# A hybrid decoder block on one core: the first shift and scale as products of raw weight blocks, and finer steps in the plan

## The chip, the cores and the metric

The kernel runs on one core of a Trainium2 chip. The metric is the device time of one execution in microseconds (us); lower is better. The kernel before took 2522.41 us, the median of 3 runs (2518.33 to 2524.78). Engines are named as the profile does: PE is TensorE (products and transposes), DVE is VectorE, ACT is ScalarE, POOL is GpSimd, and SP issues the DMA transfers.

## The reference

One layer of a decoder: 1024 tokens, 1024 channels, all in float32.

```python
mod = (silu(c) @ w_ada + b_ada)[:, None, :]            # w_ada: 1024 x 6144
sh1, sc1, gt1, sh2, sc2, gt2 = split(mod, 6)
h = rms_norm(x, norm1_w) * (1 + sc1) + sh1
q, kv, nsa_g, z, xbc, dt_raw, mg = split(h @ w_in, IN_OFFSETS)
o_attn = nsa_attention(q, kv...)      # 16 heads, 2 K/V groups: compressed, selected and window branch
o_ssm  = mamba2_mixer(z, xbc, dt_raw) # causal convolution of 4 taps over xbc, then the state space model
x = x + gt1 * ((g_attn * (o_attn @ w_attn_out) + g_ssm * (o_ssm @ w_ssm_out)) @ w_o)
h = rms_norm(x, norm2_w) * (1 + sc2) + sh2
x = x + gt2 * ((silu(h @ w_gate) * (h @ w_up)) @ w_down)   # w_gate, w_up: 1024 x 2816
return rms_norm(x, norm_f_w)
```

## The kernel before, in words

**Products.** To keep float32 accuracy a large product is taken as three: each operand is split into a high part (`hi`, a copy in the type fp32r) and a low part (`lo`, the rest), and `mm3k` issues hi·hi, hi·lo and lo·hi (L322 to L324). Making a `hi` costs an ACT copy, making a `lo` a subtraction on DVE or POOL. A few small products, and the transposes, use plain float32.

**Plan.** No engine's order is written by hand. `Flow` works out, while the program is built, when every operation would start. Each operation is queued with an engine, a cost in us, what it needs, and a function that issues it. `advance` takes from the queues of ACT, DVE, POOL and SP whatever can start first; `drive` does so for PE, choosing among streams (Python generators that yield one PE step at a time) the one that can start earliest, the first in the list at a tie. An entry whose function issues several instructions puts them in its engine's order together, with nothing between them. `first=True` puts an entry at the head of its queue. A change of one cost or one entry can thus move operations elsewhere. Buffers come from rings (`buf`, `until`): a buffer's next user waits for the operations named in `until`.

**Start.** `startup` loads the token tiles x (`xload`, eight of 512 KB), the blocks of `w_ada` that hold the first shift and scale (`wada`: halves h = 0 and 1 of the columns, eight blocks of 128 rows each), and the first weights (`split`: a raw block of 512 KB, then hi and lo). Only the SP queue sets the transfers' order: x0, x1, the eight blocks of half 0, the first raw block of kv0 (columns of w_in for keys and values), the eight blocks of half 1, the second raw block of kv0, x2, x3, kv1, x4, x5, constants, x6, x7. DVE multiplies each arriving block by its entry of `sc` = silu(c) and adds it to `acc` (L449); when a half is summed, PE adds over the partitions by products with a tile of ones (`shift_scale`, L500, two steps of four products for each half), and DVE adds the bias (`ab`, L503). `norm1` takes the norm of a pair of token tiles and transposes it (L535). `modulate` applies shift and scale to a pair's transposed quarter (`tmp`), and casts it to hT_hi and hT_lo. `token_block` then makes kv and q: eight steps of three products for a token tile and a weight block (`tokps`), pairs of tiles in order. The later tiles x4 to x7 are loaded where blocks 4 to 7 of half 1 lay.

**Middle.** Attention takes 16 units for each K/V group; its PE steps come first, and `background` fills what is left of PE with the other projections (28 weight blocks: z, x and the merge gates), with their own convolution. For the x columns `finish_x` copies the product to `xr`, and applies the taps: one ACT operation and three on DVE (`conv`, L1165, one entry). `score_cmp` is the softmax of the compressed branch, with entries of three DVE, four ACT and three DVE instructions. `value_step` transposes probabilities and copies them as a hi and lo pair (`kv`, L2321 on ACT and L2322 on DVE), with which PE makes `o` (L1098). `w_sums` prepares sums of w_down blocks, stored to DRAM.

**Towards the FFN.** `out_proj` makes x + ..., tile by tile; `norm2` stores the tile to DRAM (`x1d`), takes its norm (the root on DVE, L293 to L296 and L269, L274), and `turn_x` transposes it and makes the sums of tokens and channels for the FFN (T1 to T4). The FFN's products are taken by a scheme of seven products for a 2 x 2 block product (`gate_up`, tiles `gu`), which needs seven sums of blocks of w_gate (or w_up) as hi and lo: `ff_raw` loads two raw blocks of 512 KB, `ff_pieces` makes the sums (L1772) and `part` their hi and lo (L1753 on ACT, L1755 on DVE or POOL). Products 1 and 2 need only what even token tiles give; 3 and 5 to 7 need the odd ones. For the first pair of columns (b = 0) pieces of w_gate come before the first product, pieces 1 and 2 of w_up through `ff_first`, and the rest of w_up at the fifth product (`n == 4`). Buffers named x1r, whi_pc and wlo_pc hold the pieces; M and E hold the tokens' blocks.

## Time and profile before

| | us |
|---|---|
| median of the runs | 2522.41 |
| the profiled execution | 2519.45 |
| its span, first to last instruction | 2517.6 |
| what lies around the span | 1.85 |
| PE's longest wait, for the first x tile (L535 for DVE's L525) | 17.4 |
| PE's waits for DVE's `kv` (L1098 and L1095 for L2322), 12 together | 12.4 |
| PE's waits for DVE's `sm` (L2233 for L2238), 3 together | 4.3 |
| PE's waits for `ab` (L500 for L503), 2 together | 2.4 |

The span is that of the profiled execution alone. A row of a timeline gives start, duration, engine, line, operation, output and inputs, how many instructions stand together, and in brackets the idle time before and what ended it. A row of a table by stage gives the stretch, its length, and for each engine the busy time with its number of instructions. PEclk (in tenths) and the granted clock (1.00 is full) are TensorE's; PEld are weight loads, which run beside the products. A wait row reads: who, waited for whom: us in total, times, the longest.

### The profile page before, as it was taken

How to read it: one execution, taken by the hardware profiler on the slowest of the kernel's cores; microseconds unless marked ns; L12 is line 12 of the kernel's file. 1: busy time of each engine (PE TensorE's matmuls, PEld its weight loads, DVE VectorE, ACT ScalarE, POOL GpSimd, SP SyncE). 2: the span in 40 equal slices, each digit the busy share in tenths (PEclk: the TensorE clock that was granted, in tenths of full speed). 3: DMA queues.
4: the chain of work that ended last, by engine and by line, in shares of the span. 5: the costliest groups of instructions: out<-in, count | busy, mean ns of one | idle time of the engine just before them, and what ended most of it. 6: DMA issues, size and time to landing. Idle time of an engine off the chain costs nothing. (4 is left out here: it accounts for less than half of the span.)

```text
span 2517.6 us, 39576 instructions
## 1 busy us (share of the span) xinstructions
PE 2432.4 (97%) x13674; PEld 2080.2 (83%) x13674; DVE 1794.7 (71%) x3910; ACT 1239.0 (49%) x2644; POOL 1165.1 (46%) x924
## 2 busy tenths in 40 slices
PE   5999999999999999999999999999989999999998
PEld 5999778898888888988877778778978888887886
DVE  7644787877776687875467886778787676765858
ACT  4422666666655576655556555532453323323543
POOL 2112474645555556455634342201255565665853
PEclk8999999999999999999999999999999999999999
DMA  7432443322335433333357876426422332326853
GB/s 251 131 125 86 152 120 95 92 92 89 98 103 167 128 114 97 93 105 101 99 188 231 263 233 193 148 73 227 150 80 96 109 105 92 110 91 235 309 167 117
DMA packets 267464, 349.74 MB, mean 139 GB/s; under 512 B 21368, under 2 KB 177784, under 8 KB 266752
## 3 DMA queue, kind: packets, MB, share of 16 engines
q1 hardware_dynamic: 267264, 347.21, 42.9%
q8 instruction: 108, 1.77, 0.3%
q14 instruction: 92, 0.75, 0.1%
HBM read 249.23 MB, written 97.91 MB: 138 GB/s over the span
## 5 line engine op out<-in xcount | busy, mean ns | idle before, releaser
L2251 POOL TENSOR_SCALAR P<-P,sm,gate 128x640 f32<-128x640 f32 (+7 forms) x256 | 215.4, 856 | 246.6 <-DVE sm L2248 200.0
L2322 DVE TENSOR_TENSOR kv<-tp,kv 128x512 fp32r<-128x512 f32 (+1 forms) x296 | 189.6, 656 | 108.9 <-ACT kv L2321 107.8
L2321 ACT ACTIVATE kv<-tp 128x512 fp32r<-128x512 f32 (+1 forms) x296 | 164.9, 573 | 185.5 <-PE tp L2318 177.6
L2242 ACT ACTIVATE P<-P,sm 128x640 f32<-128x640 f32 (+7 forms) x256 | 186.9, 732 | 47.2 <-DVE sm L2238 43.3
L1098 PE MATMUL o<-kv 128*128 128x512 f32 x528 | 189.4, 411 | 13.5 <-DVE kv L2322 9.4
L2233 PE MATMUL S<-kv,Q 128*128 128x384 f32 (+5 forms) x768 | 182.8, 337 | 4.3 <-DVE sm L2238 4.3
L2238 DVE CUSTOM_DVE_ANT_0 P<-S,kb 128x256 f32<-128x256 f32 (+5 forms) x256 | 120.3, 494 | 56.7 <-PE tp L2318 29.1
L322 PE MATMUL fps<-hT_hi,whi_x 128*128 128x512 f32 x384 | 157.7, 411 | 0.1
L1165 DVE SCALAR_TENSOR_TENSOR u<-xr,hcw,u 128x512 f32<-128x512 f32 x144 | 147.4, 1024 | 13.2 <-ACT u L1168 8.3
L2318 PE MATMUL tp<-id,P 128*128 128x128 f32 x1056 | 152.7, 273 | 0.6 <-POOL P L2251 0.6
L1887 DVE TENSOR_TENSOR ex<-ex,gu 128x512 f32<-128x512 f32 x122 | 82.0, 683 | 98.4 <-PE gu L324 95.4
L322 PE MATMUL fps<-whi_z,hT_hi 128*128 128x256 f32 x512 | 149.8, 293 | 1.5 <-DVE zu L1222 1.5
L324 PE MATMUL fps<-hT_hi,wlo_x 128*128 128x512 f32 x384 | 151.2, 394 | 0.0
L323 PE MATMUL fps<-hT_lo,whi_x 128*128 128x512 f32 x384 | 151.2, 394 | 0.0
L2318 PEld LDWEIGHTS tp<-id,P 128*128 128x128 f32 x1056 | 127.9, 141 | 21.2 <-POOL P L2251 0.8
L323 PE MATMUL fps<-wlo_z,hT_hi 128*128 128x256 f32 x512 | 144.4, 282 | 0.0
L324 PE MATMUL fps<-whi_z,hT_lo 128*128 128x256 f32 x512 | 144.4, 282 | 0.0
L2233 PEld LDWEIGHTS S<-kv,Q 128*128 128x128 f32 x768 | 128.3, 190 | 19.2 <-ACT P L2242 3.1
L1098 PEld LDWEIGHTS o<-kv 128*128 128x128 f32 x528 | 95.8, 189 | 35.1 <-DVE kv L2322 17.0
L1753 ACT ACTIVATE x1r<-ex 128x512 fp32r<-128x512 f32 x115 | 70.6, 626 | 104.7 <-POOL ex L1772 31.4
L1755 DVE TENSOR_TENSOR x1r<-ex,x1r 128x512 fp32r<-128x512 f32 x89 | 108.0, 1224 | 13.9 <-ACT x1r L1753 13.7
L2392 POOL TENSOR_TENSOR dx<-xs,hd 128x512 f32<-128x512 f32 x32 | 41.8, 1308 | 162.9 <-DVE yy L2434 124.5
(490 smaller groups left out, 8036.0 us busy)
## 6 DMA issues: line engine op xcount, KB each, us to landing
wada<-w_ada SPq DMA_DIRECT2D x40, 512.0 KB, 4.2
ex<-actd SPq DMA_DIRECT2D x70, 256.0 KB, 3.7
actd<-ex SPq DMA_DIRECT2D x69, 256.0 KB, 2.0
ac<-acd SPq DMA_DIRECT2D x32, 512.0 KB, 4.8
raw_x<-w_in SPq DMA_DIRECT2D x24, 512.0 KB, 4.3
ws<-w_down SPq DMA_DIRECT2D x44, 256.0 KB, 3.6
wsd<-ws SPq DMA_DIRECT2D x88, 128.0 KB, 1.8
ff<-w_gate SPq DMA_DIRECT2D x22, 512.0 KB, 5.0
```

The costliest lines, as they stand in the source:

```text
L322: mm(ps, lh, rh, start=k == 0, stop=False)
L323: mm(ps, lh, rl, start=False, stop=False)
L324: mm(ps, ll, rh, start=False, stop=k == kt - 1)
L1098: nc.tensor.matmul(o.t.rearrange("p h q -> p (h q)"), vst(), pair()[m], start=n + m == 0, stop=n == u.total - 1 and m == 1)
L1165: nc.vector.scalar_tensor_tensor(u.t, xr[:, k:k + N2], hcw[:, ft, k:k + 1], u.t, op0=OP.mult, op1=OP.add)
L2233: mm(sp[:, :w], q, kvb.kv[:, br, r, first + c0:first + c1], start=r == 0, stop=r == 1)
L2238: nc.vector.tensor_tensor_reduce(P[:, c0:c1], sp[:, :w], k.kb[:, m0:m0 + w], scale=-1.0, scalar=sm[:, 0, h:h + 1] if p else 3.0e38, op0=OP ...
L2242: ex = A(0.26 + 0.8333e-3 * n, [mx], lambda: nc.scalar.activation(P[:, :n], P[:, :n], AF.Exp, bias=sm[:, 1, h:h + 1], scale=-1.0, accum_ou ...
L2251: nc.gpsimd.tensor_scalar(P[:, :n], P[:, :n], sm[:, 3, m:m + 1], k.gate[:, i, self.h0 + m, br + 1:br + 2], op0=OP.mult, op1=OP.mult)
L2318: nc.tensor.transpose(tp[:, h * 128:h * 128 + 128], P, k.id)
L2321: hi = A(0.064 + 0.104 * n, [op, pair], lambda: nc.scalar.activation(pair()[0][:, c], tp[:, c], AF.Copy))
L2322: lo = V(0.068 + 0.133 * n, [hi], lambda: nc.vector.tensor_sub(pair()[1][:, c], tp[:, c], pair()[0][:, c]))
```

## The change

**Start.** The accumulation on DVE and ACT is gone. PE now takes products of each raw block of w_ada as it lands: eight of 128x128 weights (the block) with one moving column (`sc` of these rows), added up over the eight blocks of a half in one PSUM tile; DVE adds bias and norm weight once for each half. x2 and x3 are loaded before half 1 of w_ada instead of behind it: the SP order is x0, x1, half 0, kv0's first block, x2, x3, half 1, kv0's second block, kv1. kv0's second `lo` and the quarter p = 0, q = 0 of hT_lo move from POOL to DVE (`fast=2`; `if q == 1 and p`). `token_block` is cut into streams for pair 0, pair 1 and pairs 2 and 3, so that kv1's pair 0 can go before kv0's pair 1.

**Single operations.** The three taps of the convolution become three entries of the plan; so do the DVE and ACT operations of `score_cmp`.

**FFN.** The 14 first pieces (seven each of w_gate and w_up for b = 0) are made during the projections, after the weight blocks 21 and 22 of `background` (`ff_save`), and stored to DRAM (`pcd`, 28 stores of 256 KB); `gate_up` loads them (`ff_saved`, 28 loads). `ff_first` and the special case in `ff_pieces` go. The x1 store is put at the head of SP's queue.

PE's order at the start; adac is the tile of shift and scale, acc the sums, xT transposed tokens, wada and the like the raw blocks, tokps the token products. Before:

```order
L535 MATMUL xT<-id,xa 128x128 x12
L500 MATMUL adac<-ones,acc_125 128x64 x4
L535 MATMUL xT<-id,xa 128x128 x4
L500 MATMUL adac<-ones,acc_125 128x64 x4
L322 MATMUL tokps<-whi_kv_169,hT_hi 128x256
L323 MATMUL tokps<-wlo_kv_180,hT_hi 128x256
L324 MATMUL tokps<-whi_kv_169,hT_lo 128x256
```

After:

```order
L483 MATMUL adac<-sc,wada_116 128x1 x32
L521 MATMUL xT<-id,xa 128x128 x4
L483 MATMUL adac<-sc,wada_116 128x1 x16
L521 MATMUL xT<-id,xa 128x128 x4
L483 MATMUL adac<-sc,wada_116 128x1 x16
L521 MATMUL xT<-id,xa 128x128 x8
L483 MATMUL adac<-sc,wada_whi 128x1 x8
L322 MATMUL tokps<-whi_kv_231,hT_hi 128x256
L323 MATMUL tokps<-wlo_kv_245,hT_hi 128x256
L324 MATMUL tokps<-whi_kv_231,hT_lo 128x256
```

Half 0's products stand first now, with the transposes of tiles 0 and 1 among them. Of half 1, single blocks of eight products alternate with single token steps of three until half 1's eighth block; four steps in all come before its last 32 products. Before, L500 of half 1 (eight products) stood behind the first four steps.

DVE's order in attention, at the first head group of the first unit; u and xr are the convolution's buffers, Q the query tile, P and sm a branch's probabilities and sizes. Before:

```order
L1174 COPY tl<-xr 128x3
L1165 SCALAR_TENSOR_TENSOR u<-xr,hcw,u 128x512 x3
L1181 SCALAR_TENSOR_TENSOR u<-xr,u 128x512
L1178 COPY xr<-tl 128x3
L1165 SCALAR_TENSOR_TENSOR u<-xr,hcw,u 128x512 x3
L2196 TENSOR_TENSOR Q_0_0_2945<-tq_0_0_2935,Q_0_0_2945 64x256
L2197 TENSOR_TENSOR Q_0_0_2945<-tq_0_0_2935,Q_0_0_2945 64x256
L1181 SCALAR_TENSOR_TENSOR u<-xr,u 128x512
```

After:

```order
L1171 SCALAR_TENSOR_TENSOR u<-xr,u 128x512
L1166 COPY xr<-tl 128x3
L1153 SCALAR_TENSOR_TENSOR u<-xr,hcw,u 128x512
L2219 TENSOR_TENSOR Q_0_0_3032<-tq_0_0_3022,Q_0_0_3032 64x256
L2220 TENSOR_TENSOR Q_0_0_3032<-tq_0_0_3022,Q_0_0_3032 64x256
L1153 SCALAR_TENSOR_TENSOR u<-xr,hcw,u 128x512
L2261 ISA P_0_0_3072,sm_0_0_3027<-S_0_0_3063,kb 128x128
L2261 ISA sm_0_0_3027 128x1
L1153 SCALAR_TENSOR_TENSOR u<-xr,hcw,u 128x512
```

The taps stood as a block of three ahead of the query's operations; now the query and the first size stand between them.

DVE's order just before the FFN's first products; rq_n is a tile's root, ops and x_7 the output projection of tile 7, wlo_pc and x1r the low parts of FFN pieces. Before:

```order
L293 TENSOR_SCALAR rq_n_19712<-rq_n_19712 128x1
L294 TENSOR_SCALAR rq_n_19712<-rq_n_19712 128x1
L1755 TENSOR_TENSOR wlo_pc<-ex,whi_pc 128x512
L1622 TENSOR_TENSOR ops<-ops,sl 128x256
L1755 TENSOR_TENSOR wlo_pc<-ex,whi_pc 128x512
L1624 TENSOR_TENSOR x_7_18751<-x_7_18751,ops 128x256
L1755 TENSOR_TENSOR x1r_19760<-ex,x1r_19760 128x512
L1755 TENSOR_TENSOR x1r_19767<-ex,x1r_19767 128x512
L1622 TENSOR_TENSOR ops<-ops,sl 128x256
L296 TENSOR_SCALAR rq_n_19712<-rq_n_19712 128x1
```

After:

```order
L293 TENSOR_SCALAR rq_n_19892<-rq_n_19892 128x1
L294 TENSOR_SCALAR rq_n_19892<-rq_n_19892 128x1
L296 TENSOR_SCALAR rq_n_19892<-rq_n_19892 128x1
L269 TENSOR_SCALAR rq_n_19892<-rq_n_19892 128x1
L274 SCALAR_TENSOR_TENSOR rq_n_19892<-rq_n_19892 128x1
L1614 TENSOR_TENSOR ops<-ops,sl 128x256
```

Four low parts stood between the root's second and third steps; now the root's steps stand together.

The diff, cut to its core:

```diff
-                E, eng, cost = (V, nc.vector, 1.14) if fast and k0 == 0 else (G, nc.gpsimd, 2.3)
+                E, eng, cost = (V, nc.vector, 1.14) if fast and k0 < 4 * fast else (G, nc.gpsimd, 2.3)
...
+        self.ada, self.adaread = [[], []], [[Op() for _ in range(8)] for _ in range(2)]
...
                 raw = lambda b=b, m=m: b[:, m].rearrange("p (j c) -> p j c", j=2)
-                d = D(1.46, [b], lambda raw=raw, k=k: nc.sync.dma_start(
-                    raw(), w[k * 128:(k + 1) * 128, 0:2, 512 * h:512 * h + 512]))
-                if k == 0:
-                    e = A(1.04, [d, e, acc], lambda raw=raw: nc.scalar.activation(acc.t, raw(), AF.Copy, scale=self.sc[:, 0:1]))
-                    self.adaread[h].append(e)
-                    continue
-                n = 256 if k == 7 else 512
-                for c0 in range(0, 512, n):
-                    x = V(0.13 + 2.08e-3 * n, [d, e], lambda raw=raw, k=k, c0=c0, n=n: nc.vector.scalar_tensor_tensor(
-                        acc[:, :, c0:c0 + n], raw()[:, :, c0:c0 + n], self.sc[:, k:k + 1], acc[:, :, c0:c0 + n],
-                        op0=OP.mult, op1=OP.add))
-                    if k == 7:
-                        self.accop[h].append(x)
-                self.adaread[h].append(x)
-                if k < 7:
-                    e = x
+                self.ada[h].append((raw, D(1.46, [b], lambda raw=raw, k=k: nc.sync.dma_start(
+                    raw(), w[k * 128:(k + 1) * 128, 0:2, 512 * h:512 * h + 512]))))
             if h == 0:
...
+        def rest():
+            xload(2)
+            xload(3)
+            wada(1)
         xload(0)
         xload(1)
         wada(0)
-        self.blocks["kv", 0] = self.split(self.win(C_KV, 256), 8, 256, "kv0", between=lambda: wada(1))
-        xload(2)
-        xload(3)
+        self.blocks["kv", 0] = self.split(self.win(C_KV, 256), 8, 256, "kv0", fast=2, between=rest)
         self.blocks["kv", 1] = self.split(self.win(C_KV + 256, 256), 8, 256, "kv1")
...
-            acc = self.acc[h]
-            for q in range(2):
-                ps = self.buf("o", [128, 2, 2, 64], "adac")
-                k = slice(4 * h + 2 * q, 4 * h + 2 * q + 2)
-                def mm(q=q, acc=acc, ps=ps):
-                    for j in range(2):
-                        for c in range(2):
-                            o = (2 * q + c) * 128
-                            nc.tensor.matmul(ps[:, j, c], acc[:, j, o:o + 128], self.ones[:, 0:64], start=True, stop=True)
...
-                op = yield ([self.accop[h][q], ps], 1.72, mm)
-                self.abop.append(V(0.27, [op], add, first=True))
-                ps.until(self.abop[-1])
-            acc.until(op)
+            ps = self.buf("o", [128, 2, 4, 1], "adac")
+            for n, (raw, d) in enumerate(self.ada[h]):
+                def mm(n=n, raw=raw, ps=ps):
+                    for c in range(4):
+                        for j in range(2):
+                            nc.tensor.matmul(ps[:, j, c], raw()[:, j, c * 128:c * 128 + 128], self.sc[:, n:n + 1],
+                                             start=n + c + j == 0, stop=n * c * j == 21)
+                op = yield ([d, self.scop] + ([ps] if n == 0 else []), 1.1, mm)
+                self.adaread[h][n].end = op.end
+            def add(ps=ps, k=slice(4 * h, 4 * h + 4)):
+                nc.vector.tensor_tensor(ab[:, :, k], ps[:, :, :, 0], bias[:, :, k], op=OP.add)
+                nc.vector.scalar_tensor_tensor(ab[:, 1, k], ab[:, 1, k], 1.0, vec[:, V_N1 + k.start:V_N1 + k.stop],
+                                               op0=OP.add, op1=OP.mult)
+            x = V(0.27, [op], add, first=True)
+            self.abop += [x, x]
+            ps.until(x)
...
-            if q == 1 or p == 0 and q == 0:
+            if q == 1 and p:
...
-                      + [Stream(self.token_block(kd, b)) for kd, b in (
-                          ("kv", 0), ("kv", 1))] + [Stream(self.token_blocks())])
+                      + [Stream(self.token_block("kv", b, ps)) for b in range(2) for ps in ([0], [1], [2, 3])] + [Stream(self.token_blocks())])
...
-        for t0 in range(0, NT, 2):
+        for t0 in (2 * p for p in pairs):
...
-        W.until(op)
-        self.next_weights()
+            W.uses.append(op)
+        if len(W.uses) == 4:
+            W.until(*W.uses)
+            self.next_weights()
...
-            def conv():
-                for k in range(3):
-                    nc.vector.scalar_tensor_tensor(u.t, xr[:, k:k + N2], hcw[:, ft, k:k + 1], u.t, op0=OP.mult, op1=OP.add)
+            def conv(k):
+                return lambda: nc.vector.scalar_tensor_tensor(u.t, xr[:, k:k + N2], hcw[:, ft, k:k + 1], u.t, op0=OP.mult, op1=OP.add)
...
-            c = V(2.5, [a0, a1, e], conv)
+            c = V(0.83, [a0, a1, e], conv(0))
+            for k in (1, 2):
+                c = V(0.83, [c], conv(k))
...
+                elif (n, q) in ((NFF - 1, 3), (NFF, 2)):
+                    self.ff_save(n - NFF + 1)
...
-        d = D(1.46, self.x1op[t], lambda: nc.sync.dma_start(self.x1d[t], self.x1[t].t))
+        d = D(1.46, self.x1op[t], lambda: nc.sync.dma_start(self.x1d[t], self.x1[t].t), first=True)
...
-    def ff_first(self, q):
...
+    def ff_save(self, q):
+        nc = self.nc
+        A, V, G, D = self.ops()
+        (r0, d0), (r1, d1) = self.ff_raw(q, 0)
+        ds = [d0, d1]
+        A11, A21, A12, A22 = (lambda r=r, m=m: r[:, :, 128 * m:128 * m + 128] for r in (r0, r1) for m in range(2))
+        def piece(n, src, need):
+            hi, lo = (self.buf(tg, [128, 4, 128], f"f{tg}{q}{n}", FR) for tg in ("c1", "c3"))
+            x = A(0.52, [need, hi], lambda: nc.scalar.activation(hi.t, src(), AF.Copy))
+            x = V(0.6, [x, lo], lambda: nc.vector.tensor_tensor(lo.t, src(), hi.t, op=OP.subtract))
+            def store():
+                for r, b in enumerate((hi, lo)):
+                    nc.sync.dma_start(self.pcd[q, n, r].bitcast(F), b.t.rearrange("p k c -> p (k c)").bitcast(F))
+            d = self.pcop[q, n] = D(1.46, [x], store)
+            hi.until(d)
+            lo.until(d)
+            return x
+        def add(need, o, x, y, op=OP.subtract):
+            return V(0.6, need, lambda: nc.vector.tensor_tensor(o(), x(), y(), op=op))
+        p1, p2, p4 = piece(1, A11, ds[0]), piece(2, A12, ds[1]), piece(4, A22, ds[1])
+        s1 = add([p4, ds[0]], A22, A21, A22, OP.add)
+        p5 = piece(5, A22, s1)
+        s3 = add([s1], A21, A11, A21)
+        p7 = piece(7, A21, s3)
+        s2 = add([s3, p1], A11, A22, A11)
+        p6 = piece(6, A11, s2)
+        s4 = add([s2, p2], A12, A12, A11)
+        p3 = piece(3, A12, s4)
+        r0.until(p6, p7, s4)
+        r1.until(p5, p3, s2)
+    def ff_saved(self, q, n):
+        p = self.piece()
+        def load():
+            for r in range(2):
+                self.nc.sync.dma_start(p.t[r].bitcast(F), self.pcd[q, n, r].bitcast(F))
+        return p, self.ops()[3](1.46, [p, self.pcop[q, n]], load)
...
-        pieces = {(0, 0): self.ff_pieces(self.ff_raw(0, 0))}
-        first = self.ff_first(1)
+        pieces = {(0, q): {} for q in range(2)}
+        saved = [(0, 1), (1, 1), (0, 2), (1, 2), (0, 3), (0, 6), (1, 3), (0, 7), (1, 6), (0, 5), (1, 7), (1, 5), (0, 4), (1, 4)]
+        for q, n in saved:
+            pieces[0, q][n] = self.ff_saved(q, n)
         while any(w.i is None for w in (self.wo[5].hi, self.wo[5].lo)):
...
-            if n == 4:
-                pieces[0, 1] = self.ff_pieces(self.ff_raw(1, 0), first)
...
         op = yield ([self.qop, k.ckcop, k.cvcop, S], 0.43, product)
         self.Q.until(op)
-        x = V(1.24, [op, P], size)
+        x = V(0.42, [op, P], lambda: nc.vector.tensor_tensor(P.t, S[:, :, 0], mask(), op=OP.add))
+        x = V(0.41, [x], lambda: nc.vector.tensor_tensor(P.t, P.t, S[:, :, 1], op=OP.add))
         S.until(x)
-        y = A(1.34, [x], expo)
-        self.P[2, 0] = P, V(0.8, [y], scale)
+        x = V(0.41, [x], lambda: nc.vector.tensor_reduce(st[:, 0], P.t, axis=AX, op=OP.max, negate=True))
+        ys = [A(0.335, [x], expo(h)) for h in range(4)]
+        self.P[2, 0] = P, V(0.4, [V(0.4, ys, root)], scale)
```

More of the change, by code (lines that the diff above doesn't have):

```diff
@@ L227, in __init__, with until @@
     def __init__(self, hi, lo):
[L228 to L232 removed]
+        self.hi, self.lo, self.ops, self.uses = hi, lo, [], []
+    def until(self, *ops):
+        self.hi.until(*ops)
+        self.lo.until(*ops)
 class Halves:
@@ L648, in token_blocks, with token_block @@
             yield from self.token_block("q", b)
-    def token_block(self, kd, b):
+    def token_block(self, kd, b, pairs=range(4)):
         W = self.blocks[kd, b]
-        for t0 in range(0, NT, 2):
+        for t0 in (2 * p for p in pairs):
             ps = self.buf("s", [128, 2, 256], "tokps")
@@ L1763, in ff_pieces @@
         A12, A22 = (lambda m=m: r1[:, :, 128 * m:128 * m + 128] for m in range(2))
-        out, early = dict(first or {}), first is not None
-        X, Y = ("V", V) if early else ("G", G)
-        pc = {n: self.piece() for n in (1, 6, 2, 7, 5, 4, 3) if n not in out}
+        out = {}
+        pc = {n: self.piece() for n in (1, 6, 2, 7, 5, 4, 3)}
         rows = {n: self.row() for n in (6, 7, 5, 3)}
@@ L1783, in ff_pieces @@
         out[5] = pc[5], self.part(pc[5], S1, s1, "V")
-        s4 = add(Y, [s2, rows[3]], S4, A12, S2)
-        out[4] = pc[4], self.part(pc[4], A22, d1, X)
+        s4 = add(G, [s2, rows[3]], S4, A12, S2)
+        out[4] = pc[4], self.part(pc[4], A22, d1, "G")
         out[3] = pc[3], self.part(pc[3], S4, s4, "V")
@@ L1790, in ff_pieces @@
         rows[3].until(out[3][1])
-        ones = [out[n][1] for n in (1, 2) if n in pc]
+        ones = [out[n][1] for n in (1, 2)]
         r0.until(s1, s2, s3, *ones)
@@ L1842, in gate_up @@
         st = {}
-        pieces[0, 1] = first
         self.gates = {}
```

51 lines of the change are left out of this document (13 added, 38 removed).

## The prediction

> **What bounds the kernel now.** I read the page's busy shares and its forty slices first:
>
> ```profile
> span 2517.6 us, 39576 instructions
> PE 2432.4 (97%) x13674; PEld 2080.2 (83%) x13674; DVE 1794.7 (71%) x3910; ACT 1239.0 (49%) x2644; POOL 1165.1 (46%) x924
> PEclk8999999999999999999999999999999999999999
> ```
>
> TensorE (PE) is busy for 2432.4 of 2517.6 us, so at most 85 us of idle time are to be had without taking work from it. The edits leave its products alone, except in the first 50 us. So the question is which idle stretches they shorten, and the next view is busy time by stage (span, PE with its instructions, weight loads, DVE, ACT, POOL, clock, DMA share, GB/s):
>
> ```profile
> 0.00:10.00 10.00, 0.00 (x0) 0.00 (x0) 2.30 (x13) 4.94 (x7) 0.73 (x5) 1.00 0.81 279
> 10.00:20.00 10.00, 2.62 (x13) 2.62 (x14) 9.93 (x17) 2.02 (x2) 0.00 (x0) 1.00 1.06 383
> 20.00:30.00 10.00, 5.92 (x29) 4.92 (x28) 7.95 (x9) 4.64 (x8) 4.66 (x3) 0.76 1.05 384
> 30.00:40.00 10.00, 5.96 (x24) 4.96 (x22) 9.82 (x11) 4.41 (x6) 6.52 (x3) 0.50 1.06 378
> 40.00:50.00 10.00, 9.39 (x57) 8.76 (x58) 8.45 (x25) 5.28 (x9) 2.49 (x1) 0.72 0.52 155
> 60.00:80.00 20.00, 19.59 (x164) 19.06 (x162) 16.74 (x62) 11.99 (x27) 2.75 (x2) 1.00 0.05 16
> ...
> 250.00:400.00 150.00, 139.18 (x733) 115.14 (x732) 120.33 (x283) 98.07 (x260) 86.27 (x92) 0.99 0.46 138
> 400.00:550.00 150.00, 145.83 (x980) 131.61 (x979) 119.95 (x291) 100.36 (x230) 78.20 (x73) 1.00 0.28 83
> 550.00:700.00 150.00, 147.66 (x931) 130.97 (x931) 110.06 (x246) 92.66 (x190) 77.56 (x67) 1.00 0.33 97
> 700.00:850.00 150.00, 143.26 (x939) 128.56 (x939) 104.42 (x243) 84.78 (x220) 82.55 (x85) 0.99 0.41 128
> 850.00:1000.00 150.00, 148.24 (x951) 131.97 (x950) 107.50 (x257) 93.77 (x224) 91.99 (x89) 1.00 0.38 116
> 1095.00:1290.00 195.00, 194.49 (x1015) 162.12 (x1014) 101.79 (x255) 107.15 (x223) 102.33 (x78) 1.00 0.35 110
> ...
> 1850.00:1860.00 10.00, 8.49 (x47) 6.64 (x46) 9.26 (x30) 6.33 (x12) 1.51 (x2) 1.00 0.48 157
> 1860.00:1870.00 10.00, 9.07 (x40) 6.92 (x39) 10.00 (x11) 7.88 (x15) 9.31 (x6) 1.00 0.01 2
> 1870.00:1880.00 10.00, 4.87 (x17) 2.87 (x16) 9.90 (x11) 3.77 (x7) 8.19 (x6) 0.93 0.18 49
> ```
>
> PE idles 50 - 23.9 = 26.1 us in the first 50 us (DMA saturated at about 384 GB/s, clock at half for much of it), 750 - 724.2 = 25.8 us from 250 to 1000, and 30 - 22.4 = 7.6 us from 1850 to 1880, where DVE is full. From 1095 to 1290, with attention going on but no convolution, it idles 0.5 us.
>
> **Part 1, the first shift and scale on PE.** The rows that carry it (start, duration, engine, what, and in brackets the idle time before and what ended it):
>
> ```profile
> 9.60 1.28 DVE L449 SCALAR_TENSOR_TENSOR acc<-wada,sc,acc 128x1024 f32<-128x1024 f32 x1 [0.52 <-DMA wada<-w_ada]
> 19.13 1.06 ACT L351 ACTIVATE whi_kv<-raw_kv 128x1024 fp32r<-128x1024 f32 x1 [2.42 <-DMA raw_kv<-w_in]
> 32.77 1.06 ACT L520 ACTIVATE jk<-xa 128x1024 f32<-128x1024 f32 x1 [0.23 <-DMA xa<-x]
> 17.38 2.82 PE L535 MATMUL xT<-id,xa 128*128 128x128 f32 x12 [17.38 <-DVE xa L525]
> 20.00 1.81 PE L500 MATMUL adac<-ones,acc 128*128 128x64 f32 x8
> 23.84 1.10 PE L500 MATMUL adac<-ones,acc 128*128 128x64 f32 x8 [1.58 <-DVE ab L503]
> 36.03 1.97 PE L500 MATMUL adac<-ones,acc 128*128 128x64 f32 x8 [0.81 <-DVE ab L503]
> L500 PEld LDWEIGHTS adac<-ones,acc x32: 186/333/338, 19.8 to 37.5; 128*128 128x128 f32 x32
> L535 PE MATMUL xT<-id,xa 128*128 128x128 f32 x32 | 5.5, 333 | 17.4 <-DVE xa L525 17.4
> 1281.44 1.89 PE L2419 MATMUL yd<-xs,E 128*128 128x64 f32 x16
> 1283.17 1.08 PE L2450 MATMUL sp<-xw,bdm 128*128 128x512 f32 x2
> ```
>
> From the second half's arrival at 19.13 to token tile 2 at 32.77 lie ten transfers of 512 KB: 1.36 us each. So in the new order tiles 2 and 3 land near 20.5 and 21.8, 12 us earlier, and all w_ada blocks by about 33.
>
> An f32 product is two passes: L500 has 16 matmuls and 32 records. With 64 moving columns 16 passes take 1283.17 - 1281.44 = 1.73 us, 0.108 each, and weights are reloaded for every pass. The new ones load 128x128 weights for one moving column, which no row shows. From below the bound is the DMA: a block per 1.36 us. From above it is the cold pass: (1.81 - 0.33) / 7 = 0.21 us. I take 0.108, the nearest row with 128 weight columns per pass. The change has 16 blocks x 8 matmuls x 2 = 256 passes: 27.6 us on PE where 32 stood. A block costs 1.73 us, more than the 1.36 us in which it arrives: **PE, not DMA or DVE, becomes the start's bound.**
>
> By the Trainium skill's "TensorE: Matmul & The Clock Gate", section "Back-to-back issue gap", weight load and matmul pairs of 128 columns are sustained at about 81 ns; by that figure the 256 passes would take an estimated 20.7 us. The 0.108 us row disagrees with it for f32, and the row decides my sum.
>
> Now the chain. PE starts when block 0 lands, one step before the row at 9.60: near 8.1. Up to the last block its new order has 256 passes (27.6 us), 20 transposes at about 0.12 (2.4), 12 token products at 0.12 (1.4; 19.59 us for 164 gives 0.12). The clock was still half at 20.00-21.8 (8 passes in 1.81 us) and full at 23.84 (8 in 1.10): it opened about 4.2 us after PE's first work at 17.38. Two microseconds are lost to that, and 0.6 while PE waits for the first hT. Together: 8.1 + 27.6 + 2.4 + 1.4 + 2 + 0.6 = 42, against 38.0 (36.03 + 1.97) now. Behind it come ab, tmp, the cast and the DVE share of wlo, about 4 us, in which PE has only 12 transposes and 6 products (2.1 us); so it idles 2 us and then streams from about 46.5. By 50 it has done 18 + 3.5 / 0.12 = 47 token products; before, 123 records - 32 - 32 = 59. Twelve are 1.4 us; if the idle stretch closes the clock, 1 to 2 more. **Term: +2.5 us, own range -1 to +6.** The 20 us of DVE work that go hide nothing here: PE waited for DVE's ab, and now waits for itself. DVE takes the POOL pieces (wlo, one hT_lo) in the room that leaves: nothing. The later tiles 4 to 7 wait for PE's reading of the blocks in xa, and SP holds the constants, kv1's second half and the gate columns behind them; tile 7 lands near 45 (43.6 now by the same spacing), and its first reader comes after 60 us: nothing, or 2 us if PE is late.
>
> **Part 2, single operations.** What stands ahead of the waits for DVE:
>
> ```profile
> PE o L1098 <- DVE kv L2322: 9.1, 8, 2.7
> 745.96 4.63 DVE L1165 SCALAR_TENSOR_TENSOR u<-xr,hcw,u 128x512 f32<-128x512 f32 x3
> 750.51 1.27 DVE L2322 TENSOR_TENSOR kv<-tp,kv 128x512 fp32r<-128x512 f32 x2
> 751.25 1.15 PE L1098 MATMUL o<-kv 128*128 128x512 f32 x3 [2.74 <-DVE kv L2322]
> ```
>
> The convolution's three operations stand as one entry, 4.63 us here, and the kv piece that PE needs stands behind. Eight waits of this kind cost 9.1 us from 250 to 1100, and other waits there hang on DVE too. Apart, the entry holds a ready operation up for a third of that. From 1095, where no convolution runs, 195 us have 0.5 us of idle. That bounds the gain by the 25.8 us. But the plan's order is new for the whole stage, so other accidents come: I take half of the 9.1, **-5 us, range -10 to +4.** The split compressed softmax is in the same term. The saved pieces' work (22 DVE, 14 ACT operations, 28 stores) falls where 1095-1290 shows DVE busy 101.8 of 195: nothing, or 1 us if that cover were gone.
>
> **Part 3, the first FFN pieces from DRAM.** The rows around the switch:
>
> ```profile
> 1846.74 0.15 DVE L294 TENSOR_SCALAR rq_n<-rq_n 128x1 int32<-128x1 int32 x1
> 1852.71 0.14 DVE L296 TENSOR_SCALAR rq_n<-rq_n 128x1 int32<-128x1 int32 x1
> 1872.45 0.50 PE L323 MATMUL gu<-E,x1r 128*128 128x512 f32 x1 [2.01 <-DVE E L1700]
> 1875.72 1.75 DVE L1772 TENSOR_TENSOR ex<-ff,ex 128x512 f32<-128x512 f32 x1
> 1878.18 0.50 PE L322 MATMUL gu<-M,x1r 128*128 128x512 f32 x1 [2.89 <-ACT x1r L1753]
> 1878.52 0.58 PE L323 MATMUL gu<-M,x1r 128*128 128x512 f32 x1
> 1882.02 0.39 PE L324 MATMUL gu<-M,x1r 128*128 128x512 f32 x1
> ```
>
> Tile 5's root stands still on DVE from 1846.74 to 1852.71 behind low pieces; then the second matrix's sums and pieces keep DVE full, and PE waits 2.01 and 2.89 us for them. Ten products take 3.84 us from 1878.18 instead of 10 x 0.235, 1.5 us lost to the clock after the wait. All these pieces become loads. What is late next is the last tiles' own chain (root, transpose, T1 to T3): with DVE free it starts 1.5 us earlier or more, and four products that need only even tiles (4 x 12 x 0.235 = 11 us) cover it. SP issues the 28 loads between the x1 stores, 256 KB each; 14 products take 14 x 2.8 = 39 us, DMA is at 0.01 to 0.48 there. Of 7.6 + 1.5 us I leave 1: **-8 us, range -9 to -4.** The x1 store put first in SP's queue changes nothing that PE waits for.
>
> **Sum.** 2.5 - 5 - 8 = -10.5 us. The profiled execution took 2519.45 us (its span and 1.85 around it); the median shown, 2522.41, is 3 us above. 2519.45 - 10.5 = 2509 in the profile's terms, **2512 us** as a median. Its own range, with the terms' ends taken half together: 2503 to 2520. About 0.3% (7.6 us) is what a measurement can tell here.
>
> **The rivals.** (a) *The clock stays half through the one-column products.* They stream almost nothing through the array. For it: between 30 and 40 us PE is busy 5.96 of 10 us and the clock stays 0.50. Against it: it opened after transposes and 64-column passes, which also stream only part of the time, as soon as PE was busy without a gap. The same page, section "Part 4: PE-mode transpose", says that transposes do not count as busy for the clock gate; here it opened 4.2 us after a start with twelve transposes, so the trace does not bear that out, but that not every instruction counts is the danger. Price: 256 x 0.214 = 54.8, 20 x 0.2, 12 x 0.21, so the last block ends at 8.1 + 61.3 = 69.5. By then 59 + 19.5 / 0.12 = 220 token products were done before, and 12 are now: 25 us lost. Total 25 - 13 = +12: **2535 us**. It decides from about half: if more than 60% of the passes run cold, the kernel is slower. (b) *A one-column pass is cheaper*, 0.08 us or less: the last block ends near 35 and the start gains 5 to 8 us instead of losing 2.5: **2503 us**. For it: nothing streams; against it: passes of 64 columns, which stream half of what 128 would, are bound by the load already. (c) *The new order brings as many waits as it removes* from 250 to 1000, Part 2 at +4: 2521, no change that can be measured; this is the end of the forecast's own case. (d) *The pieces come late from DRAM*: PE then waits at its first gu product; 5 us of Part 3 back, 2517; the loads' place in SP's queue speaks against it.
>
> **How the numbers follow.** The forecast with (c) and (d): 0.57; (a): 0.30; (b): 0.13. In the first, two thirds to three quarters lie over 7.6 us faster, the rest within; (a) is slower but for a tenth; (b) is faster. Faster 0.54, same 0.19, slower 0.27. The range must reach into (a) and (b): 2501 to 2538; it leaves out the lower part of (b) and the upper part of (a).
>
> **What would show it.** Right: adac records in runs of 16 per block at 0.108 us from about 8 us, the last near 42; PEclk at full from about 13; PE idle under 2 us from 1850 to 1880; fewer waits "o <- DVE kv" with convolutions ahead. Wrong: PEclk at 0.50 until 60 or later (a); adac blocks spaced 1.36 us with PE idle between them (b); idle time from 250 to 1000 at 25 us or more (c).

## The result and the profile after

The changed kernel took 2553.47 us, the median of 5 runs (2544.98 to 2557.88), against 2518.33 for the kernel before (5 runs, 2516.09 to 2524.78): a ratio of 1.0129 (95% interval 1.0113 to 1.0145), about 32 us slower. The forecast was 2512, with a range of 2501 to 2538. The profiled execution took 2553.47 us, with a span of 2551.7.

The page's head and clock row of the changed kernel:

```profile
span 2551.7 us, 40144 instructions
PE 2482.6 (97%) x13898; PEld 2132.3 (84%) x13898; DVE 1768.0 (69%) x3901; ACT 1238.0 (49%) x2642; POOL 1155.1 (45%) x913
PEclk9999999999999999999999999999999999999999
```

PE has 224 records more (256 block passes for 32), but 50.2 us more busy time: 0.22 us for each. Its idle time fell from 85.2 to 69.1 us. So the time was not lost in waits. Next three stages of the first 100 us (same columns as before), and PE's rows in that time (start, duration, engine, line, operation, output and inputs, records together):

```profile
10.00:20.00 10.00, 10.00 (x49) 10.00 (x49) 1.02 (x4) 1.81 (x2) 0.00 (x0) 1.00 1.06 388
30.00:40.00 10.00, 10.00 (x50) 10.00 (x48) 1.47 (x3) 2.30 (x5) 0.00 (x0) 1.00 0.38 127
50.00:60.00 10.00, 10.00 (x49) 10.00 (x49) 0.00 (x0) 0.00 (x0) 0.00 (x0) 1.00 0.05 7
```

```profile
8.27 13.79 PE L483 MATMUL adac<-sc,wada 128*128 128x1 f32 x64 [8.27 <-DVE rq_n L293]
21.91 1.09 PE L521 MATMUL xT<-id,xa 128*128 128x128 f32 x4
...
69.27 1.95 PE L521 MATMUL xT<-id,xa 128*128 128x128 f32 x8
...
74.87 0.39 PE L322 MATMUL tokps<-whi_kv,hT_hi 128*128 128x256 f32 x1 [1.71 <-DVE hT_hi L558]
...
77.17 0.58 PE L324 MATMUL tokps<-whi_kv,hT_lo 128*128 128x256 f32 x1 [1.79 <-DVE hT_lo L563]
...
82.67 0.41 PE L322 MATMUL tokps<-whi_kv,hT_hi 128*128 128x256 f32 x1
82.88 0.37 PE L323 MATMUL tokps<-wlo_kv,hT_hi 128*128 128x256 f32 x1
...
83.21 0.28 PE L322 MATMUL tokps<-whi_kv,hT_hi 128*128 128x256 f32 x1
```

PE is busy without a gap from 8.27 to 72 us, DVE stands nearly still, and DMA, full before until 40 us, has little to do from about 34 to 58: PE bounds the start, as forecast. But a pass takes (21.91 - 8.27) / 64 = 0.213 us, and the last block ends at 69.3. The token products are as slow, 0.41 us in most of their rows until 82.9; then 0.28. The clock was at half for nearly all of that time. It opened for a moment near 75 (the product at 75.09 takes 0.28), and the column of the granted clock, 1.00 up to 76, reads 0.50 from 77 to 83. For the first 70 us its 1.00 can't be right: an experiment below shows the same pace with 0.50 beside it. In the runs here the column read 1.00 wherever the clock had not changed since the start, so it is not to be believed for a kernel's first stretch.

Where the 34.1 us of the two spans lie, by the start of some products (each from the tile's own listing in the trace; "first fps" is the first product of the projections behind the token blocks, "last o" the last of attention, gu the FFN's):

| start of, us | before | after | start alone | without the start |
|---|---|---|---|---|
| first fps | 250.3 | 285.0 | 283.9 | 250.3 |
| last o | 1271.2 | 1308.4 | 1298.0 | 1262.2 |
| first gu | 1850.8 | 1891.2 | 1879.2 | 1842.3 |
| last gu | 2292.3 | 2326.6 | 2321.2 | 2279.8 |
| span | 2517.6 | 2551.7 | 2546.5 | 2504.6 |

The start costs 34.7 us. From first to last gu the kernel gains 6.1 (441.5 us, now 435.4).

The theory: *a stream of one-column products does not count as work for the clock, which therefore stayed at half.* Rivals: a pass over a raw block has a price of its own, 0.21 us, at any clock (B); products bound by their weight load, or by data just arrived, do not count however wide they are (C); a clock once open stays open, only its start is missing (D).

### The profile page after: what moved, and what is told of

Same layout as the page of the kernel before. It is cut to its first block, busy times and chain, and to the rows that moved or that the text cites. A ratio compares the mean times of both kernels' runs of the same rounds, so it can differ in the third digit from the quotient of the medians.

```text
span 2551.7 us, 40144 instructions
## 1 busy us (share of the span) xinstructions
PE 2482.6 (97%) x13898; PEld 2132.3 (84%) x13898; DVE 1768.0 (69%) x3901; ACT 1238.0 (49%) x2642; POOL 1155.1 (45%) x913
## 4 chain that ended last, share of the span: by engine, by line
PE 79%; DVE 11%; DMA 4%; ACT 3%; issue 2%; POOL 1%; SPq 0%; ACTq 0%; DVEq 0%; POOLq 0%
PE fps L322 7%; PE fps L324 7%; PE fps L323 7%; PE gu L323 5%; PE gu L322 5%; PE gu L324 5%; PE o L1087 4%; PE S L2256 4%; PE tp L2340 4%; PE dps L324 2%; PE dps L323 2%; PE dps L322 2%; PE adac L483 2%; PE sps L322 2%; PE sps L324 2%
## 5 line engine op out<-in xcount | busy, mean ns | idle before, releaser
L2274 POOL TENSOR_SCALAR P<-P,sm,gate 128x640 f32<-128x640 f32 (+7 forms) x256 | 228.7, 904 | 282.7 <-DVE sm L2271 198.2
L2261 DVE CUSTOM_DVE_ANT_0 P<-S,kb 128x256 f32<-128x256 f32 (+5 forms) x256 | 121.6, 494 | 53.1 <-PE tp L2340 34.7
L1153 DVE SCALAR_TENSOR_TENSOR u<-xr,hcw,u 128x512 f32<-128x512 f32 x144 | 137.2, 956 | 11.8 <-ACT u L1156 8.3
L1745 ACT ACTIVATE x1r<-ex 128x512 fp32r<-128x512 f32 x102 | 62.9, 627 | 117.7 <-POOL ex L1763 60.4
L322 PE MATMUL fps<-hT_hi,whi_m 128*128 128x512 f32 x256 | 113.0, 441 | 0.0
```

The source lines that it names most:

```text
L322: mm(ps, lh, rh, start=k == 0, stop=False)
L1153: return lambda: nc.vector.scalar_tensor_tensor(u.t, xr[:, k:k + N2], hcw[:, ft, k:k + 1], u.t, op0=OP.mult, op1=OP.add)
L2261: nc.vector.tensor_tensor_reduce(P[:, c0:c1], sp[:, :w], k.kb[:, m0:m0 + w], scale=-1.0, scalar=sm[:, 0, h:h + 1] if p else 3.0e38, op0=OP ...
L2274: nc.gpsimd.tensor_scalar(P[:, :n], P[:, :n], sm[:, 3, m:m + 1], k.gate[:, i, self.h0 + m, br + 1:br + 2], op0=OP.mult, op1=OP.mult)
```

## The experiments

Ratios are to the kernel before, run beside each kernel on the same chip, with 95% intervals; its medians there were 2519.31 to 2519.8 us.

**The start alone, and all but the start.** The kernel before with the change of startup, shift_scale, modulate and token_block alone:

> The kernel before with the change's start alone (products of raw w_ada blocks, the new transfer order, the streams by pairs); convolution, compressed softmax and FFN pieces as before. Theory: the whole loss lies in the start, +34.7 us at the first product of the projections behind attention: 2551 to 2556. Rival (the other parts lose too, the start less): under 2545.

The changed kernel with these as before:

> The changed kernel with the start of before; single operations and saved FFN pieces as changed. Theory: by the milestones of the two traces attention gains 4 us until the convolution ends and loses 6 behind it, 3 more are lost up to the FFN, and 6 come back there: -1 us, 2512 to 2520, no change that can be measured. Forecast on record for these two parts: -13 us, 2505. Rival (the late order of the plan was made bad by the late start): 2506 to 2511.

Measured: 2549.05 us, 1.0118 (1.0103 to 1.0133), for the start alone; 2511.78 us, 0.9974 (0.9962 to 0.9985), without it. The start alone costs what the whole change costs; the rest, with the old start, is a small gain, less than the -13 us of the record and more than the theory's -1. This last beats both kernels; so does a version below, with the single operations alone.

**64 moving columns instead of one.**

```diff
-            ps = self.buf("o", [128, 2, 4, 1], "adac")
+            ps = self.buf("o", [128, 2, 4, 64], "adac")
...
-                            nc.tensor.matmul(ps[:, j, c], raw()[:, j, c * 128:c * 128 + 128], self.sc[:, n:n + 1],
+                            nc.tensor.matmul(ps[:, j, c], raw()[:, j, c * 128:c * 128 + 128], self.sc[:, n:n + 1].to_broadcast([128, 64]),
```

> The changed kernel with 64 moving columns, all the same, instead of one in each product of a w_ada block. Theory A (a stream of one-column products does not count as work for the clock): with 64 the clock opens within 5 us of the first products, a pass takes 0.108 us, the last product of half 1 ends at 42 to 45 us, total 2520 to 2527. Rival C (products bound by their weight load do not count, however many columns move) or rival B (a pass over a raw block takes 0.21 us at any clock): last product near 69 us, total 2550 to 2556.

Measured: 2543.07 us, 1.0087 (1.0061 to 1.0112); its six runs spread from 2530.79 to 2549.47, so the profiled one (2549.47) may not speak for all. The last blocks in it:

```profile
61.78 1.06 PE L521 MATMUL xT<-id,xa 128*128 128x128 f32 x4
62.64 6.93 PE L483 MATMUL adac<-sc,xa 128*128 128x64 f32 x32
```

The last product ends at 69.4 (69.36 is the start of the next row), a pass takes (69.36 - 62.64) / 32 = 0.21 us. Theory A, as it stood, is wrong: in this execution 64 columns were not enough either. The six runs lie in two groups, three from 2547.21 to 2549.47 and three from 2530.79 to 2538.93, so 64 may be near the bound, and the clock may have opened earlier in the faster three; no trace of those was kept.

**The clock opened beforehand**, by 24 products of a tile of ones ahead of the first block (their result isn't used):

```diff
+        wp = self.buf("s", [128, 512], "warm")
...
+            for _ in range(24):
+                nc.tensor.matmul(wp[:, 0:128], self.ones, self.ones, start=True, stop=True)
```

> The changed kernel with 24 products of a tile of ones (128 moving columns) ahead of the first block, so that the clock is open when the one-column products begin; their result is not used. Theory A: passes run at 0.11 us or less at first, the clock falls back within some 10 us of one-column products, and the last product of half 1 ends at 60 to 67 us: 2544 to 2552. Rival B (a pass takes 0.21 us at any clock): 0.21 from the first pass, with transposes between them at 0.12. Rival D (once open, the clock stays open): the last product ends at 35 to 42 us, total 2513 to 2522.

Measured: 2537.39 us, 1.0075 (1.0062 to 1.0089). The block products of this run by stage (PE with its records, weight loads, DVE, clock, DMA share, GB/s):

```profile
8.00:12.00 4.00, 3.55 (x33) 3.66 (x33) 0.00 (x0) 1.00 1.05 394
12.00:16.00 4.00, 4.00 (x21) 4.00 (x20) 0.00 (x0) 0.50 1.05 385
20.00:24.00 4.00, 4.00 (x21) 4.00 (x20) 0.00 (x0) 0.50 1.03 388
```

With the clock open a one-column pass takes 3.55 / 33 = 0.108 us, the row that the prediction chose; B falls. After 3.5 us of such passes (from 8.45 to 11.97) the clock falls to 0.50 and stays there, with no gap on PE; D falls. 128 columns had opened it: 48 passes of the tile of ones took 7.4 us, so some 21 of them 0.213 and the rest 0.107. The page "TensorE: Matmul & The Clock Gate" of the Trainium skill, section "Part 1: The HAM clock gate", has the clock follow the PE's activity in windows of about 3.4 us. The 3.5 us until it fell agree with that. What counts as activity that section of the Trainium skill doesn't say, and here it is not the presence of instructions. The last block product ends at 66.1, as the theory expected; the total is below the theory's 2544 to 2552, which the last part of this section takes up.

**128 and 96 moving columns.** The moving operand is silu(c)'s entry and 127 (95) zeros, the outputs overlap by all but one column, and two products with zeros start the bank:

```diff
+        zp = self.buf("a1", [128, 8, 128], "zp")
+        z = G(0.5, [zp], lambda: nc.gpsimd.memset(zp.t, 0.0))
+        z = V(0.1, [z, self.scop], lambda: nc.vector.tensor_copy(zp[:, :, 0], self.sc))
...
+                            nc.tensor.matmul(ps[:, 4 * j + c:4 * j + c + 128], raw()[:, j, c * 128:c * 128 + 128], zp[:, n],
```

> The changed kernel with 128 moving columns in each product of a w_ada block: the entry of silu(c), then 127 zeros, so that eight results stand side by side in one bank and the zeros add nothing. The run with 64 columns showed the clock at half up to 71 us and 0.21 us a pass, and the run with the products of ones showed that 128 columns open it. Theory A in its new form (what counts is the share of time in which columns stream; 64 of the 256 clocks of a cold pass are too few, 128 are enough): the clock opens by 14 us, a pass takes 0.107, the last product of half 1 ends at 41 to 45 us, and the total is that of the run without the new start plus 2 to 6: 2513 to 2519. Rival C in its new form (products of blocks just arrived from DRAM, or a stream with a new weight in every pass, do not count, however wide): last product near 69 us, total 2543 to 2553.

> As with 128 moving columns, but 96 (the entry, then 95 zeros): 96 of the 256 clocks of a cold pass. With 64 the clock stayed shut, with 128 it opened. If the bound lies under 0.375 of the time: opens by 15 us, last product at 44.5 us, total as with 128, 2519 to 2524. If it lies above: shut up to 69 us, 2543 to 2553.

Measured: 2521.58 us, 1.0005 (0.9995 to 1.0016), with 128; 2525.89 us, 1.0023 (1.0011 to 1.0036), with 96. PE's rows with 128 columns:

```profile
8.34 9.62 PE L489 MATMUL adac<-zp,wada 128*128 128x128 f32 x64 [5.58 <-DVE rq_n L294]
...
18.23 3.74 PE L489 MATMUL adac<-zp,wada 128*128 128x128 f32 x32
...
40.97 3.74 PE L489 MATMUL adac<-zp,xa 128*128 128x128 f32 x32
...
50.15 0.39 PE L322 MATMUL tokps<-whi_kv,hT_hi 128*128 128x256 f32 x1 [3.22 <-DVE hT_hi L565]
...
52.44 0.58 PE L324 MATMUL tokps<-whi_kv,hT_lo 128*128 128x256 f32 x1 [1.78 <-DVE hT_lo L570]
```

and the block products by stage with 96:

```profile
8.00:12.00 4.00, 3.77 (x18) 3.80 (x19) 0.00 (x0) 1.00 1.05 397
12.00:16.00 4.00, 4.00 (x31) 4.00 (x31) 0.00 (x0) 1.00 1.05 388
16.00:20.00 4.00, 3.73 (x35) 3.67 (x34) 0.00 (x0) 1.00 1.07 383
```

From 18 records in 4 us to 31, then 35: the clock opens within 6 us of the first block, in both runs, and half 1's last product ends near 44.6. C falls, and the theory stands in a new form: *what counts is the share of time in which columns stream.* A cold pass lasts 0.213 us with 1, 64 or 128 columns; if 128 of them fill half of it (an estimate: a cold token product of 256 columns takes the same 0.213), 64 fill a quarter and 96 three eighths, and the bound lies between those two, as far as the one trace with 64 shows. A cold pass lasts the same here whatever its width, so these runs can't tell the share of time from the number of columns in a pass. The full columns save 2553.47 - 2521.58 = 32 us of the loss, 25.3 of them up to the first fps, though not all: it comes at 259.7, 9.4 us later than before.

**Which part of the start costs the 9 us.** The new transfer order and the streams by pairs, with DVE summing as before (on the kernel without the new start), and the reverse, products with 128 columns in the old order:

> The run without the new start, with the new order of transfers alone (x2 and x3 ahead of half 1 of w_ada, and the streams by pairs), DVE summing the blocks as before. Theory: the second half of shift and scale comes 2.7 us later, and PE has tiles 2 and 3 to transpose in between but no product of theirs to make without it: 0 to +3 us against the run without the new start, 2511 to 2515. Rival (the early tiles fill the idle time of the start): 2506 to 2509.

> The run with 128 moving columns, with x2 and x3 loaded behind half 1 of w_ada as before and the token products of a weight in one stream. In the run with 128 columns the clock was open from 15 us, and the first product of the projections behind attention still came 9.4 us later than before; in the run with the early tiles alone 9.1 us later. Theory: the order of the transfers and tiles costs most of the 9 us whichever engine sums the blocks; without it that product comes 0 to 4 us later than before (250 to 255 us), total 2511 to 2517. Rival: PE's 27 us of block products cost it, and the early tiles only when DVE sums: 257 to 261 us, total 2518 to 2523.

Measured: 2522.19 us, 1.0008 (0.9995 to 1.0021), first fps at 259.4; 2526.22 us, 1.0018 (1.0005 to 1.0031), first fps at 265.8. Both expectations of the theory missed. By the first fps the early tiles alone cost 9.1 us where 0 to 3 were expected; the block products alone cost 15.5 where 0 to 4 were. Together they cost 9.4: the early tiles are bad for DVE's sums and good for PE's, and neither half of the change is a gain. Where it goes with 128 columns is seen behind the last block, DVE first (start, duration, line, what), then two stages:

```profile
44.74 0.17 DVE L496 TENSOR_TENSOR ab<-adac,vec 128x8 f32<-128x8 f32 x1 [1.19 <-PE adac L489]
...
45.14 0.99 DVE L553 TENSOR_SCALAR tmp<-xT,ab 128x256 f32<-128x256 f32 x2
46.05 1.22 DVE L353 TENSOR_TENSOR wlo_kv<-raw_kv,whi_kv 128x1024 fp32r<-128x1024 f32 x1
47.18 2.91 DVE L565 CAST hT_hi<-tmp 128x512 fp32r<-128x512 f32 x2
```

```profile
40.00:50.00 10.00, 6.93 (x61) 6.50 (x59) 6.88 (x10) 6.38 (x11) 2.75 (x2) 1.00 0.66 198
50.00:60.00 10.00, 8.07 (x47) 7.86 (x48) 9.04 (x28) 3.66 (x9) 3.60 (x2) 0.66 0.50 154
```

The last block is 6.5 us later than before. Behind it the chain of ab, tmp, a low part of kv0 (both of them are on DVE now, not only the first) and the casts leaves PE idle for 3.22 and 1.78 us, and the clock closes again, from 50.6 to 57.4 (0.66 from 50 to 60, 47 records where before had 83).

**Single operations one by one**, on the kernel before: both, the convolution's three entries alone, the softmax's entries alone.

> The kernel before with the single operations alone (convolution and compressed softmax). Record: -5 us (-10 to +4). From the run without the new start, which gained 6.6 us with this and the saved pieces together: theory, the gain lies in the FFN: 2516 to 2520. Rival, it lies in attention: 2511 to 2515.

> The kernel before with the convolution's three entries alone, the compressed softmax as before. The run with both gained 0.37% (0.23 to 0.52). Theory (the waits for kv behind a convolution were the cause): most of it, 2510 to 2515. Rival (the softmax's entries carry half or more, or the plan's luck does): 2516 to 2520.

> The kernel before with the compressed softmax's single entries alone, the convolution as one entry. With both 0.37% (0.23 to 0.52) were gained, with the convolution alone 0.17% (0.06 to 0.28) lost, and there the longest wait for kv had the softmax's entry of three ahead of it. Theory (each of the two entries stands in the way when the other is gone): about as before, 2516 to 2522, with waits for kv of over 2 us behind a convolution. Rival (the softmax's entries alone bring the gain): 2508 to 2514, and waits for kv under 3 us in all.

Measured: both together 2513.41 us, 0.9963 (0.9948 to 0.9977), so the rival was right and the gain lies in attention (PE idles 14.7 us from 250 to 1000, against 25.8); the convolution alone 2525.68, 1.0017 (1.0006 to 1.0028), and the softmax alone 2537.07, 1.0066 (1.0048 to 1.0085), both above every range that was expected. PE's waits for kv in attention (us in total, times, longest) with both, and with the softmax alone:

```profile
PE o L1098 <- DVE kv L2322: 1.8, 6, 0.4
```

```profile
PE o L1098 <- DVE kv L2321: 14.4, 9, 4.2
```

With the softmax alone, DVE ahead of the longest of these waits:

```profile
342.58 3.53 DVE L1165 SCALAR_TENSOR_TENSOR u<-xr,hcw,u 128x512 f32<-128x512 f32 x3
346.03 0.68 DVE L1181 SCALAR_TENSOR_TENSOR u<-xr,u 128x512 f32<-128x512 f32 x1
346.64 0.68 DVE L2321 TENSOR_TENSOR kv<-tp,kv 128x512 fp32r<-128x512 f32 x1
```

and with the convolution alone:

```profile
749.73 1.05 DVE L2280 TENSOR_TENSOR st<-st,gate 128x4 f32<-128x4 f32 x1
...
750.82 2.08 DVE L2281 TENSOR_TENSOR Pc<-Pc,st 128x256 f32<-128x256 f32 x1
...
752.82 1.24 DVE L1177 COPY xr<-tl 128x3 f32<-128x3 f32 x1
...
754.16 1.27 DVE L1164 SCALAR_TENSOR_TENSOR u<-xr,hcw,u 128x512 f32<-128x512 f32 x1
...
755.35 0.68 DVE L2323 TENSOR_TENSOR kv<-tp,kv 128x512 fp32r<-128x512 f32 x1
...
756.08 1.22 PE L1098 MATMUL o<-kv 128*128 128x512 f32 x2 [2.63 <-DVE kv L2323]
```

In each of the two an entry that was left whole stands ahead of kv; with the convolution alone a copy and one tap follow it. With both cut the waits for kv are nearly gone. That a single cut loses 4 and 17 us is more than these waits explain (9.2 and 14.4 us, against 9.1 before). In the profiled executions PE is idle for 85.6 and 92.2 us, against 85.2 before, and busy for 9.0 and 7.4 us more with the same 13674 records, at a mean clock of 0.989 against 0.992: much of the loss is time at a lower clock. Each cut also moves the rest of the plan; which stretches lose the clock was not taken apart further.

**The saved pieces alone**, on the kernel before:

> The kernel before with the saved FFN pieces alone (and the x1 store first). Record: -8 us (-9 to -4): 2511. Theory: 6 us come back at the FFN and up to 4 are lost where the pieces are made: 2513 to 2518. Rival (the making costs as much as it brings): 2518 to 2522.

Measured: 2518.65 us, 0.9996 (0.9986 to 1.0005), as the rival had it: the making costs nearly what it brings. From first to last gu it gains 2.7 us (438.8), and where the pieces are made, from 1100 to 1290, PE idles 2.4 us instead of 0.5. The waits that are left at the first gu products, in the run without the new start:

```profile
PE h2T L1668 <- ACT x L1649: 2.7, 1, 2.7
PE gu L323 <- DVE M L1705: 2.1, 1, 2.1
```

The first is the last tile's transpose. Its root's steps stand on DVE between sums for other tiles, from 1845.02 to 1853.15:

```profile
1846.31 1.61 DVE L1705 TENSOR_TENSOR ex<-ex 128x512 f32<-128x512 f32 x1
1847.85 1.25 DVE L274 SCALAR_TENSOR_TENSOR rq_n<-rq_n 128x1 f32<-128x1 f32 x1
...
1850.80 1.77 DVE L1705 TENSOR_TENSOR E<-ex,E 128x512 fp32r<-128x512 f32 x1
```

Two edits of that run asked why. The root's steps at the head of DVE's queue (`first=True` in norm2's root):

> The run without the new start, with the steps of a tile's root at the head of DVE's queue. There tile 7's root took 8 us on DVE, between sums for other tiles, and PE waited 2.69 us for that tile's x and 2.12 for the M piece behind it. Theory (what is late behind the saved pieces is the last tile's own chain): those two waits fall below 2 us together, total 2 to 4 us less than without: 2508 to 2510, which the times can hardly tell and the profile can. Rival (the chain waits for the sums of other tiles anyway): the same waits within 1 us, 2512.

The sums T1 to T4 all on DVE, none on POOL (`add(G, ...)` to `add(V, ...)` in turn_x, four times):

> The run without the new start, with the sums T1 to T4 (their POOL part) on DVE. There tile 7's root stood 8 us on DVE among sums that took 1.55 to 1.77 us while POOL worked, and 0.69 else, and PE waited 4.8 us in all. Theory (POOL's work stretches DVE's, and that keeps the last tile late): with POOL idle there these operations take 0.7 us, and the waits behind the saved pieces fall to 2.5 us or less, total 2 to 3 us less than without: 2509 to 2515, which only the profile tells. Rival (DVE's own queue is what is long): the waits stay at 4 us or grow, since DVE has 4 to 6 more operations of 0.7 us for each pair.

Measured: 2516.87 us, 0.9988 (0.9975 to 1.0002), and 2516.56 us, 0.9986 (0.9974 to 0.9997), both above what was expected; the times tell neither from the run that they edit. The first left the order of the last tile's root as it was, with the same wait of 2.7 us, so it tells nothing of the theory. In the second the sums take 0.64 to 0.69 us each, and the waits fall from 4.8 to 2.7 us:

```profile
1855.65 1.28 DVE L1705 TENSOR_TENSOR ex<-ex 128x512 f32<-128x512 f32 x2
1856.85 0.69 DVE L1705 TENSOR_TENSOR M<-ex,M 128x512 fp32r<-128x512 f32 x1
```

```profile
PE gu L322 <- ACT M L1708: 2.3, 1, 2.3
PE gu L323 <- DVE M L1705: 0.4, 1, 0.4
```

So POOL's sums do stretch DVE's: 0.69 us is drawn out to 1.55 or more, and even a step of one column takes 1.25. The Trainium skill's page "Advanced Engine Details and Errata", section "GPSIMD Details", names an interface that the two share, which instructions with two inputs from SBUF contend for; the rows agree.

That POOL's sums keep the last tile late isn't shown, though. With POOL idle the root of this tile takes as long, since DVE now has all the sums between its first and its last step:

```profile
1854.36 0.14 DVE L293 TENSOR_SCALAR rq_n<-rq_n 128x1 f32<-128x1 f32 x1
...
1862.57 0.16 DVE L274 SCALAR_TENSOR_TENSOR rq_n<-rq_n 128x1 f32<-128x1 f32 x1
```

That is 8.4 us, against 8.1, and the tile's transposes start 12.2 us after the first gu product, against 12.0. PE no longer waits for them because 48 gu products stand ahead of them in its order, not 36. The 2.7 us that are left come behind the transposes.

**How far one profile reaches.** The run with the clock opened beforehand has the changed kernel's order on every engine, but for the 24 products. Attention, from first fps to last o, in the changed kernel and in that run:

```profile
285.00:1308.40 1023.40, 998.29 (x6055) 872.36 (x6054) 743.68 (x1760) 634.38 (x1460) 571.49 (x521) 0.99 0.38 119
```

```profile
282.10:1292.00 1009.90, 992.39 (x6055) 868.58 (x6054) 737.75 (x1756) 632.91 (x1460) 571.18 (x522) 1.00 0.38 120
```

The same 6055 records take 13.5 us longer in one execution: 7.6 us more of idle time, and 5.9 more of busy time at a lower clock. The run with the roots first and the one that it edits have the same DVE order up to the last tiles, and differ there by 7.2 us (1019.1 and 1011.9). What sets this was not found. A milestone in attention from one profile is worth no more than some 10 us. Nor is it chance of the profiled execution alone: all five runs of the changed kernel took 2544.98 to 2557.88 us and all five with the clock opened beforehand 2536.95 to 2540.70, though their first fps lie 2.9 us apart. So a difference of 10 us between two ratios, too, need not be the work of the edit.

## Why the prediction was wrong

**Part 1, the start: +2.5 forecast, 34.7 measured.** The step that failed is "it opened about 4.2 us after PE's first work". The prediction took that from a start with transposes of 128 columns and carried it over to a stream of one-column products. That stream leaves the clock at half for as long as it lasts. The row at 19.13 was misnamed (it is the arrival of kv0's first block, not of the second half), but the ten transfers behind it are counted rightly. The rest of the step was sound: 256 passes, 0.108 us each with an open clock (measured 0.108), 0.21 with a closed one (measured 0.213), PE as the bound. Rival (a) named the mechanism and put the last block at 69.5 (measured 69.3), but got a chance of 0.30, and its price stopped at that block. Behind it the clock opens for a moment, PE waits 1.71 and 1.79 us for hT, and the clock is at 0.50 again until 83.1. Between 69.3 and 83.1 PE does 36 token products and 12 transposes where 115 products would go at 0.12 us, an estimated further 8 to 9 us: 25 + 9 = 34. The row that spoke for (a), 0.50 at 5.96 of 10 us busy, was read as a matter of gaps. The argument against it, that the clock had opened after transposes and 64-column passes, rested on one start of 4.2 us, which can't tell which of the two opened it; with 64 columns alone it stayed shut in the profiled run.

Even in the forecast's own case the term was too small. With the clock open the start costs 9.4 us, outside -1 to +6: the last block comes at 44.6 instead of 42, PE idles 5 us instead of 2, and the clock falls once more. "If the idle stretch closes the clock, 1 to 2 more" had it, and cost it too low: from 52.4 to 57.4 PE runs at half the pace, an estimated 2.5 us.

**Part 2, single operations: -5 forecast, about -9 measured (0.9963, -13 to -6 us).** Right in sign, and the interval reaches into the forecast's range. The waits for kv went, as forecast. The reason was half of it: it is not the convolution's entry alone, since with that cut alone nothing is gained.

**Part 3, saved pieces: -8 forecast, -1 measured (0.9996, -3.5 to +1.3).** The step that failed is "Of 7.6 + 1.5 us I leave 1". The pieces did go from DVE, and come from DRAM in time, so rival (d) is out. What is late next was named, the last tiles' own chain, but it was called covered by four products. It wasn't: sums for the other tiles stand between the steps of the last tile's root on DVE and draw it out to 8 us, three of the four products (36 of 48) stand ahead of its transposes in PE's order, and 4.8 us of waits remain in the run without the new start. The making of the pieces, put at nothing, costs some 2 us of idle time.

**Sum.** The parts measured apart give 29.7 - 9.3 - 1.0 = 19 us; the change measured whole gave 32. In the changed kernel the two smaller parts bring nothing in: the start alone is at 1.0118, the whole at 1.0129. The 13 us between are not settled: two runs with the same order in attention differ by as much, and the plan is another one behind a later start.

## What to carry to other kernels

Before work is moved to TensorE, count the columns that stream, not only the passes: a product of one column took as long here as one of 128, and a long run of them kept the clock shut for everything beside it. So price such a stream at half clock, and also what follows it until wide products have run without a wait for some 6 us (77.2 to 83.1 in the changed kernel). Price waits behind it too: 3.2 and 1.8 us of them closed an open clock for 6.8 us. In a planned order, cut all long entries that stand before the waited-for operation or none, and measure each cut with enough runs, since one cut moves the whole order.
